# Moving tiles within a partition by 128 bytes, and placing the last output products by hand, in a hybrid decoder layer

## The chip, the core and the metric

The kernel is one Bass/Tile program on one core of a Trainium2 chip. The metric is the device time of one execution in microseconds (us). Five engines have work in it: TensorE (PE in the profile, with its weight loads listed apart as PEld), VectorE (DVE), ScalarE (ACT), GpSimd (POOL), and SyncE (SP), whose queue issues nearly all DMA transfers. Each engine takes its own instructions in a fixed order, which is settled when the program is built; a transfer at the head of SP's queue that has to wait holds up the ones behind it.

On-chip memory (SBUF) has 128 partitions. A tile takes the same byte range in each of them, so that "where a tile lies" is one byte address. A matmul reads two operands from there: the stationary one (128 columns, put into the array by a weight load ahead of the matmul) and the moving one (up to 512 columns, streamed through).

## What is computed

One decoder layer over x, 1024 tokens by 1024 features, float32:

```python
xn = rmsnorm(x, attn_norm_g)
proj = xn @ w_in                     # 2312 columns
# 8 sliding-window heads with sinks and ALiBi, 8 forgetting-attention heads, QK-norm in both
mixed = concatenate([out_a, out_b])  # 1024 columns
h = x + mixed @ w_out
y = h + square(relu(rmsnorm(h, mlp_norm_g) @ w_up)) @ w_down     # hidden width 4096
```

Each float32 operand of a large product is split into a high part (rounded to the type fp32r) and a low part (what is left), and each product is made of three matmuls: high by high, high by low, low by high.

## The kernel before

**Stages.** (1) Features of x come in eight blocks k; the first 384 columns of the projection are accumulated in eight PSUM banks `qps` (lines 168 to 191). (2) `load_w` brings further projection weights, `proj` makes the product `ps` of one block of 128 tokens (24 matmuls of 384 or 392 columns). The blocks are "fillers", handed out by the table `PACE` between the units of attention. (3) `heads_a` and `heads_b` run 48 attention units; a unit is a score step (`scores_a`, `scores_b`) and, two units later (`DEPTH`), a mix step (`mix_a`, `mix_b`), which transposes the probabilities, splits them (`evict_pt`) and multiplies them with the values (`pvb`). The list `marks` holds the last matmul of each score step. (4) The output product: `out_first` makes the half over e = 0 to 3 of all eight blocks dt of 128 output features while attention still runs; for dt = 0 and 4, e = 4 to 6 and then e = 7 are made at the end of attention (lines 862 to 875); the other six dt follow at lines 950 to 957. (5) `up`: 16 steps j of a Strassen-like product, seven products n of 12 matmuls of 512 columns each (`pu`). (6) `down`: 1344 matmuls of 512 columns (`pd`).

**Who sets the order.** Tile builds the program with a simulated timeline: at each step it takes the ready instruction of the highest priority. `tc.high_priority` raises what it wraps, `prep` uses it for attention; `tc.issue_after(ins)` queues what it wraps behind `ins` on that engine, which is a bound on the order and no wait; `paced()` is that with the newest mark. So an edit in one place can change the order of others.

**Where tiles lie.** The left side of memory holds the constants `cp` and behind them first x in its high and low parts (`xh`, `xl`, pool `xg_p`) with the projection weights (`wp`), later the pool `zl` (output weights, the attention outputs `mix`, up weights `wu`, part of what `down` uses). Sizes are rounded up to 32 bytes. Counted modulo 256 bytes, the constants begin at 128 and their odd-sized tiles put x and `zl` at 96. A projection weight tile has 392 floats, which is 6 times 256 bytes and 32 more, so that the eight high tiles and the eight low ones each begin 32 bytes further on, through all eight multiples of 32. The right side is filled from the end of memory: pools `ap1` and `ap2` for attention, later `zr` (the operands `bh` and `bl` of `up`, its sums, part of `down`). `zr` and its tiles lie at 224. In `ap2` small tiles stand between the large ones: q lies at 64, k and the split probabilities at 192.

**The attention outputs on their way to the output product.** `mix_b` (or `mix_a`) stores its result in `mix_d`. For each block e, `split_mix` loads it with its denominators (`mixr`, `mixn`, two tiles each), multiplies, splits into the one tile `mixs` (both parts; high on ACT, low on POOL), and stores 512 KB to `mixs_d`, once per half c. `load_mix(e)` brings the block back as `mix`. Its steps (load, half 0, half 1) are taken one per attention unit, from the units in `SPLITS`. Block e = 7 is split by `mix_b` directly.

Of the kernel before, what the change touches and what calls it, by code (L numbers as in the profile page):

```python
# [25 lines left out]
NJ = NF // 2  # L26
EPS = 1e-6
WN = 392
NW = 7
NWARM = 8  # L30
HPO = 8000
# [22 lines left out]
def hybrid_layer(  # L54
# [15 lines left out]
    def mm(out, lhsT, rhs, start, stop):  # L70
        return nc.tensor.matmul(out, lhsT, rhs, start=start, stop=stop)  # L71
# [29 lines left out]
    ones1 = cp.tile([P, 1], F32, name="ones1")  # L101
    nc.vector.memset(ones1, 1.0)

    vt = cp.tile([P, 36], F32, name="vt")
    nc.scalar.dma_start(vt, vecs)
    nc.scalar.preload_act_table_set("natural_log_exp_and_others")
    ga, gm, vec, bfb, snk = (
        vt[:, a:b] for a, b in ((0, 8), (8, 16), (16, 20), (20, 28), (28, 36))
    )
# [30 lines left out]
    at = ExitStack()  # L140
    ap1 = at.enter_context(tc.tile_pool(name="ap1", bufs=1, side="right"))
    ap2 = at.enter_context(tc.tile_pool(name="ap2", bufs=1, side="right"))
    maskd = ap2.tile([P, P], F32, tag="mt", name="maskd", bufs=2)
    nc.gpsimd.memset(maskd, 0.0)
    nc.gpsimd.affine_select(
# [4 lines left out]
    nc.vector.tensor_copy(mask_b, maskd)  # L150
    qk_t = lambda name: ap1.tile([P, NT, 384], F32, tag="qk", name=name, bufs=2)

    def w_tiles():
        return [
            wp.tile([P, WN], dt, tag=tag, name=tag, bufs=n)
            for tag, dt, n in (("wr", F32, 3), ("wh", F32R, 8), ("wl", F32R, 8))
        ]


    st0 = ExitStack()  # L160
# [6 lines left out]
    halves = [slice(c * 512, (c + 1) * 512) for c in range(2)]  # L167
    for k in range(KT):
        xr = ap2.tile([P, S], F32, tag="s", name="xr", bufs=NS)
        wr, wh, wl = w_tiles()  # L170
        nc.sync.dma_start(xr[:, halves[0]], xT[k * P : (k + 1) * P, halves[0]])
        nc.sync.dma_start(wr[:, :384], w_a0[:, k, :])
        nc.sync.dma_start(xr[:, halves[1]], xT[k * P : (k + 1) * P, halves[1]])
        split(wh[:, :384], wl[:, :384], wr[:, :384], nc.vector, nc.gpsimd if k else nc.vector)
        for cs in halves:
            nc.scalar.activation(xh[:, k, cs], xr[:, cs], AF.Copy, scale=ga[:, k : k + 1])
            nc.vector.scalar_tensor_tensor(
                out=xl[:, k, cs], in0=xr[:, cs], scalar=ga[:, k : k + 1],
                in1=xh[:, k, cs].bitcast(F32), op0=ALU.mult, op1=ALU.subtract,
            )  # L180
        passes = ((xh, wh), (xh, wl), (xl, wh))
        order = (
            [(t, j) for j in range(3) for t in range(NT)] if k == 0
            else [(t, j) for t in (range(NT) if k < KT - 1 else LAST) for j in range(3)]
        )
        for t, j in order:
            x_, w_ = passes[j]
            mm(
                qps[t][:, :384], x_[:, k, t * P : (t + 1) * P], w_[:, :384],
                k == 0 and j == 0, k == KT - 1 and j == 2,  # L190
            )
    q0 = qk_t("q0")
# [10 lines left out]
    def load_w(src, n):  # L203
        his, los = [], []
        for k in range(KT):
            wr, wh, wl = w_tiles()
            nc.sync.dma_start(wr[:, :n], src[:, k, :])
            with tc.high_priority(offset=HPO):
                split(wh[:, :n], wl[:, :n], wr[:, :n], nc.scalar, nc.gpsimd)
            his.append(wh)  # L210
            los.append(wl)
        return his, los
# [3 lines left out]
    def proj(w, n, t):  # L216
        his, los = w
        ps = pd.tile([P, 512], F32, tag="pd", name="ps")
        tsl = slice(t * P, (t + 1) * P)
        for k in range(KT):  # L220
            mm(ps[:, :n], xh[:, k, tsl], his[k][:, :n], k == 0, False)
            mm(ps[:, :n], xh[:, k, tsl], los[k][:, :n], False, False)
            pe = mm(ps[:, :n], xl[:, k, tsl], his[k][:, :n], False, k == KT - 1)
            if k == KT // 2:
                middle.append(pe.ins)
        return ps

    def qknorm(x, nh, tlo, thi, r=None):


        n = thi - tlo
        w = nh * HD
        sq = ap2.tile([P, 1024], F32, tag="sq", name="sq", bufs=1)
        sqv = sq[:, : n * w].rearrange("p (t c) -> p t c", t=n)
        xv = x[:, tlo:thi, :w]
        nc.gpsimd.tensor_tensor(out=sqv, in0=xv, in1=xv, op=ALU.mult)
        ss, r0, u = (
            ap2.tile([P, 16], F32, tag=tag, name=tag, bufs=2)[:, : n * nh]
            for tag in ("ss", "sr0", "su")
        )  # L240
        nc.vector.tensor_reduce(
            out=ss, in_=sq[:, : n * w].rearrange("p (g d) -> p g d", d=HD),
            axis=AX.X, op=ALU.add,
        )
        th = lambda a: a.rearrange("p (t h) -> p t h", h=nh)
        nc.vector.scalar_tensor_tensor(
            out=th(ss), in0=th(ss), scalar=1.0 / HD,
            in1=ep2[:, tlo:thi].unsqueeze(2).to_broadcast([P, n, nh]),
            op0=ALU.mult, op1=ALU.add,
        )  # L250
        nc.scalar.activation(r0, ss, AF.Ln)
        nc.scalar.activation(r0, r0, AF.Exp, scale=-0.5)
        nc.vector.tensor_tensor(out=u, in0=r0, in1=r0, op=ALU.mult)
        nc.vector.tensor_tensor(out=u, in0=u, in1=ss, op=ALU.mult)
        na = nh + (2 if r is not None else 0)
        if r is None:
            rv = ap2.tile([P, 16], F32, tag="r", name="r", bufs=2)[:, : n * nh]
            rv = th(rv)
        else:
            rv = r[:, tlo:thi, :]  # L260
        nc.vector.scalar_tensor_tensor(
            out=rv[:, :, :nh], in0=th(u), scalar=3.0, in1=th(r0),
            op0=ALU.subtract, op1=ALU.mult,
        )
        for t in range(n):
            xt = x[:, tlo + t, : na * HD].rearrange("p (h d) -> p h d", d=HD)
            nc.gpsimd.tensor_tensor(
                out=xt, in0=xt, in1=rv[:, t].unsqueeze(2).to_broadcast([P, na, HD]), op=ALU.mult
            )
# [153 lines left out]
    def forget_gates():  # L423
# [29 lines left out]
            off[: NH * NT, 0:1], before.rearrange("p h t -> p (h t)"),  # L453
            cum[:, P - 1 : P], True, True,
        )
        offs = ap2.tile([NH * NT, 1], F32, name="offs")
        nc.vector.tensor_copy(offs, off[: NH * NT, 0:1])
        nc.vector.tensor_scalar(
            out=cum, in0=cum, scalar1=offs[:, 0:1], scalar2=None, op0=ALU.add
# [96 lines left out]
    def split_mix(e):  # L556


        got = {}

        def load():
            for c in range(2):
                cs = slice(c * 512, (c + 1) * 512)
                m, q = got[c] = [
                    ap2.tile([P, 512], F32, tag=n, name=n, bufs=2) for n in ("mixr", "mixn")
                ]
                nc.sync.dma_start(m, mix_d[e][:, cs])
                for h in range(2):
                    nc.sync.dma_start(
                        q[rows_of[h], :], rd_d[2 * e + h, cs].partition_broadcast(HD)  # L570
                    )

        def make(c):
            m, q = got[c]
            hl = ap2.tile([P, 2, 512], F32R, tag="mixs", name="mixs", bufs=1)
            with tc.issue_after(mixed[-1]):
                nc.vector.tensor_tensor(out=m, in0=m, in1=q, op=ALU.mult)
            split(hl[:, 0], hl[:, 1], m, nc.scalar, nc.gpsimd)
            nc.sync.dma_start(
                mixs_d[e][:, :, c * 512 : (c + 1) * 512].rearrange("c p s -> p c s"),  # L580
                hl.bitcast(F32),
            )

        return [load, lambda: make(0), lambda: make(1)]

# [39 lines left out]
    def scores_b(p, qp, h):  # L625
        q1, k1, k2, cb = heads[p, "q"][h], heads[p, "k1", h], k2_of[h], heads[p, "cb", h]
        probs = []
        for i in (2 * qp, 2 * qp + 1):
# [2 lines left out]
                [P, S if i > 3 else 512], F32, tag="s" if i > 3 else "u", name="sb",  # L631
                bufs=NS if i > 3 else NU,
            )
            nm = ap2.tile([P, 4], F32, tag="nm", name="nmb", bufs=4)
            dn = ap2.tile([P, 4], F32, tag="dn", name="dnb", bufs=4)
            qs = q1[:, i * P : (i + 1) * P]
            for c in range((nk + 511) // 512):
                n = min(512, nk - c * 512)
# [32 lines left out]
    def mix_b(probs, p, qp, h):  # L671
        r = slice(h * HD, (h + 1) * HD)
        pv = pa.tile([P, 512], F32, tag="pv", name="pvb", bufs=2)
        for b in range(qp + 1):
# [18 lines left out]
            for par in range(2):  # L693
                st = heads[p, "v", h][:, 2 * b + par, :]
                mm(pvo, st, hv[:, :, 1 - par, :], b == 0 and par == 0, False)
                mm(pvo, st, lv[:, :, 1 - par, :], False, diag and par == 1)
        tmp = ap2.tile([HD, 512], F32, tag="cmb", name="tmpb", bufs=1)
        nc.scalar.copy(tmp[:, :256], pv[HD:, :256])
        mt = ap2.tile([P, 256], F32, tag="mt", name="mtb", bufs=2)
# [8 lines left out]
            split(mh[7][r, ms], ml[7][r, ms], mt[r, :], nc.scalar, nc.vector)  # L708

    qkb = {}  # L710
    mh, ml, mixt = {}, {}, {}
    pend = []

# [4 lines left out]
    def drain(n):  # L718
        while len(pend) > n:
            prep(pend.pop(0))  # L720
# [139 lines left out]
        heads_b(p)  # L860
    fill(True)
    load_mix(6)
    ahead_of = []
    for dt in (0, 4):
        w = out_weights(dt, 4)

        ps = first_banks() if dt == 0 else [
            pa.tile([P, 512], F32, tag="sc", name=f"po{c}", bufs=2) for c in range(2)
        ]
        with paced():  # L870
            out_products(ps, w, range(4, 7))
        ahead_of.append((dt, ps, w))
    drain(0)
    for dt, ps, w in ahead_of:
        out_products(ps, w, [7])

# [24 lines left out]
    def out_finish(dt, ps):  # L901
        t, gain = dt % 4, gm[:, dt : dt + 1]
        h = slot(f"w{2 + dt // 4}", "h", [S]) if dt < 7 else rr
        part["load"] = nc.sync.dma_start(h, part_d[dt])
        for c, cs in enumerate((left, right)):
            nc.vector.tensor_tensor(out=h[:, cs], in0=ps[c], in1=h[:, cs], op=ALU.add)
        nc.sync.dma_start(h_d[dt], h)
# [379 lines left out]
```

## Time and profile before

| | |
|---|---|
| median of 3 runs | 1126.16 us (1122.52 to 1127.7) |
| profiled execution | 1124.34 us, of which its span is 1122.6 us |
| granted TensorE clock, mean | 0.998 |
| matmuls | 5551, of which `pu` 1344, `pd` 1344, `ps` 960, `po` 384, `qps` 200 |

The profile is one execution. Busy time of PE is the union of its matmuls, which overlap: a matmul of 512 columns is listed with some 390 ns, but a new one starts every 230 ns or so. The rate is read from the chain of work that ended last, which merges matmuls that follow each other without a wait into one piece, with the piece's length and their number.

### The profile page before, as it was taken

The numbers are of one execution on the slowest core, as the hardware profiler recorded it, in microseconds if no ns is written. First come the engines' busy times: TensorE is split into PE (matmuls) and PEld (weight loads), VectorE is DVE, ScalarE is ACT, GpSimd is POOL, SyncE is SP. The second block draws the span as 40 slices with busy tenths as digits, with TensorE's granted clock in tenths as the row PEclk, the third lists the DMA queues.
The fourth block names the chain that finished last, engine by engine and source line by source line (L and its number), as shares of the span: only waits on it lengthen the run. The fifth ranks groups of instructions, "written<-read, shape, count | busy, mean of one in ns | idle before, by whom it ended". The sixth has DMA issues, their size and how long they took to land.

```text
span 1122.6 us, 15570 instructions
## 1 busy us (share of the span) xinstructions
PE 1098.7 (98%) x5551; PEld 937.5 (84%) x5551; DVE 765.4 (68%) x1311; ACT 575.4 (51%) x1013; POOL 361.0 (32%) x338
## 2 busy tenths in 40 slices
PE   9999998999999999899999999999999999999998
PEld 8999988799997888777888887888888888888886
DVE  7476665765667577699867677855575876674395
ACT  5567557766677656455454534344444433333331
POOL 4751613335434545124232323222221222222100
PEclk9999999999999999999999999999999999999999
DMA  9311302314438656473454544335699786665523
GB/s 312 124 36 37 95 24 59 96 29 142 153 120 312 203 182 219 168 236 131 173 194 169 196 151 159 134 121 194 227 392 351 258 299 244 216 230 205 173 95 113
DMA packets 95710, 195.68 MB, mean 174 GB/s; under 512 B 7136, under 2 KB 19088, under 8 KB 95632
## 3 DMA queue, kind: packets, MB, share of 16 engines
q1 hardware_dynamic: 95488, 194.66, 49.6%
q8 instruction: 44, 0.72, 0.3%
q14 instruction: 34, 0.28, 0.1%
q10 hardware_dynamic: 144, 0.02, 0.0%
HBM read 141.61 MB, written 53.04 MB: 173 GB/s over the span
## 4 chain that ended last, share of the span: by engine, by line
PE 83%; DVE 7%; issue 4%; DMA 4%; POOL 1%; ACT 1%; SPq 0%; DVEq 0%; ACTq 0%; POOLq 0%
PE pd L71 27%; PE pu L71 27%; PE ps L71 12%; PE po L71 4%; PE qps L71 3%; PE spb L71 3%; PE pvb L71 2%; PE tpb L683 2%; PE sp L71 1%; DVE ptl L360 1%; DMA mixs_d<-mixs 1%; DVE sb L647 1%; DVE bl L78 1%; PE pv L71 1%; DMA wr<-in_w_b_dram 1%
## 5 line engine op out<-in xcount | busy, mean ns | idle before, releaser
L71 PE MATMUL pd<-hx,wx 128*128 128x512 f32 x1344 | 304.9, 389 | 0.0
L71 PEld LDWEIGHTS pd<-hx,wx 128*128 128x128 f32 x1344 | 252.3, 188 | 52.4
L71 PE MATMUL pu<-bh,wu 128*128 128x512 f32 x896 | 281.6, 395 | 0.8 <-ACT wu L75 0.8
L71 PEld LDWEIGHTS pu<-bh,wu 128*128 128x128 f32 x896 | 168.8, 188 | 40.7 <-ACT wu L75 1.2
L71 PE MATMUL pu<-bl,wu 128*128 128x512 f32 x448 | 176.9, 395 | 0.5 <-DVE bl L78 0.5
L75 ACT CAST hx<-hr 128x1024 fp32r<-128x1024 f32 x56 | 59.0, 1054 | 176.2 <-PE pd L71 171.3
L78 POOL TENSOR_TENSOR wx<-wda,wx 128x1024 fp32r<-128x1024 f32 x24 | 64.5, 2687 | 197.0 <-ACT wx L75 197.0
L78 DVE TENSOR_TENSOR hx<-hr,hx 128x1024 fp32r<-128x1024 f32 x56 | 72.7, 1305 | 73.5 <-ACT hx L75 73.4
L71 PE MATMUL ps<-wh,xh 128*128 128x384 f32 (+1 forms) x320 | 110.2, 345 | 0.3 <-ACT qkb L600 0.3
L71 PE MATMUL ps<-wh,xl 128*128 128x384 f32 (+1 forms) x320 | 109.3, 342 | 0.0
L71 PE MATMUL ps<-wl,xh 128*128 128x384 f32 (+1 forms) x320 | 109.1, 342 | 0.0
L71 PEld LDWEIGHTS pu<-bl,wu 128*128 128x128 f32 x448 | 84.4, 188 | 21.1 <-DVE bl L78 0.9
L71 PE MATMUL po<-mix,wos 128*128 128x512 f32 x384 | 95.8, 400 | 3.7 <-DMA mix<-mixs_d 1.6
L78 POOL TENSOR_TENSOR wu<-wus,wu 128x512 fp32r<-128x512 f32 x32 | 48.0, 1501 | 133.4 <-ACT wu L75 133.4
L71 PEld LDWEIGHTS po<-mix,wos 128*128 128x128 f32 x384 | 70.9, 190 | 18.3 <-DMA mix<-mixs_d 1.8
L75 ACT CAST wu<-wus 128x512 fp32r<-128x512 f32 x64 | 39.0, 618 | 79.4 <-PE pu L71 76.0
L78 POOL TENSOR_TENSOR wu<-wur,wu 128x512 fp32r<-128x512 f32 x32 | 43.3, 1354 | 88.2 <-ACT wu L75 88.2
L360 DVE TENSOR_TENSOR ptl<-tpb,pth 128x512 fp32r<-128x512 f32 (+1 forms) x80 | 50.0, 632 | 25.9 <-ACT pth L359 25.2
L965 DVE TENSOR_TENSOR ht<-hb 128x512 f32<-128x512 f32 x32 | 21.8, 722 | 64.7 <-ACT hb L1020 64.7
L78 POOL TENSOR_TENSOR wl<-wr,wh 128x384 fp32r<-128x384 f32 (+1 forms) x47 | 49.9, 1076 | 48.8 <-ACT wh L75 36.9
L75 ACT CAST wx<-wda 128x1024 fp32r<-128x1024 f32 x56 | 58.3, 1044 | 7.2 <-DMA wda<-in_w_d_dram 6.6
L71 PEld LDWEIGHTS ps<-wh,xh 128*128 128x128 f32 x320 | 60.4, 189 | 1.1 <-ACT qkb L600 0.6
(218 smaller groups left out, 2058.4 us busy)
## 6 DMA issues: line engine op xcount, KB each, us to landing
wda<-in_w_d_dram SPq DMA_DIRECT2D x34, 1024.0 KB, 9.0
hr<-hid_d SPq DMA_DIRECT2D x56, 512.0 KB, 5.8
wur<-in_w_u_dram SPq DMA_DIRECT2D x32, 512.0 KB, 4.4
hid_d<-ht SPq DMA_DIRECT2D x16, 1024.0 KB, 4.3
hid_d<-hb SPq DMA_DIRECT2D x16, 768.0 KB, 3.6
mixs_d<-mixs SPq DMA_DIRECT2D x14, 512.0 KB, 3.4
mix<-mixs_d SPq DMA_DIRECT2D x7, 1024.0 KB, 8.7
wr<-in_w_b_dram SPq DMA_DIRECT2D x32, 192.0 KB, 2.4
```

The lines of the kernel that those rows point to most:

```text
L71: return nc.tensor.matmul(out, lhsT, rhs, start=start, stop=stop)
L75: hi_eng.copy(hi, src)
L78: lo_eng.tensor_tensor(out=lo, in0=src, in1=hi.bitcast(F32), op=ALU.subtract)
L360: nc.vector.tensor_tensor(out=lo[:, cols], in0=pt[:, cols], in1=hi[:, cols].bitcast(F32), op=ALU.subtract)
L647: nc.vector.tensor_tensor_reduce(out=pr[:, c * 512 : c * 512 + n], in0=sp[:, :n], in1=cb[:, c * 512 : c * 512 + n], scale=1.0, scalar=3e38 ...
L683: nc.tensor.transpose(tp[:, c0 : c0 + P], probs[qi][:, kb * P : (kb + 1) * P], ident)
L965: eng.tensor_tensor(out=out, in0=a, in1=b, op=ALU.subtract)
```

## The change

Seven edits:

1. `vt`, a tile of constants, grows from 36 to 68 floats. All that lies behind it on the left side moves by 128 bytes: x, the projection weights and the pool `zl` with the up weights. Modulo 256 they then begin at 224.
2. The high and low part of a projection weight go into one tile of 832 floats (13 times 256 bytes), the low one 1536 bytes behind the high one (1600 for the 392 columns of `w_a1`).
3. Small attention tiles go to a pool of their own, `ap3`, so that `ap2` holds only multiples of 256 bytes.
4. The first weight block is loaded from ACT's queue, and ACT's table load comes behind it.
5. `split_mix` writes the high part over the denominators `mixn`; `mixs` holds the low part alone, and each half is stored by two transfers.
6. At the end of attention, the products of dt = 0 and 4 over e = 4 to 6 are placed one by one behind a mark or behind the last matmul of a mix step (the list `ended`).
7. The partial sum of dt = 7 is loaded behind that of the block before it.

```diff
+WL = 416
...
-    vt = cp.tile([P, 36], F32, name="vt")
-    nc.scalar.dma_start(vt, vecs)
-    nc.scalar.preload_act_table_set("natural_log_exp_and_others")
+    vt = cp.tile([P, 68], F32, name="vt")
+    nc.scalar.dma_start(vt[:, :36], vecs)
...
+    ap3 = at.enter_context(tc.tile_pool(name="ap3", bufs=1, side="right"))
...
-    def w_tiles():
-        return [
-            wp.tile([P, WN], dt, tag=tag, name=tag, bufs=n)
-            for tag, dt, n in (("wr", F32, 3), ("wh", F32R, 8), ("wl", F32R, 8))
-        ]
+    def w_tiles(n):
+        w = wp.tile([P, 2 * WL], F32R, tag="w", name="w", bufs=8)
+        wr = wp.tile([P, WN], F32, tag="wr", name="wr", bufs=3)
+        lo = 384 if n == 384 else 400
+        return wr[:, :n], w[:, :n], w[:, lo : lo + n]
...
-        nc.sync.dma_start(wr[:, :384], w_a0[:, k, :])
+        (nc.sync if k else nc.scalar).dma_start(wr, w_a0[:, k, :])
+        if k == 0:
+            nc.scalar.preload_act_table_set("natural_log_exp_and_others")
...
-            ap2.tile([P, 16], F32, tag=tag, name=tag, bufs=2)[:, : n * nh]
+            ap3.tile([P, 16], F32, tag=tag, name=tag, bufs=2)[:, : n * nh]
...
                 m, q = got[c] = [
-                    ap2.tile([P, 512], F32, tag=n, name=n, bufs=2) for n in ("mixr", "mixn")
+                    ap2.tile([P, 512], dt, tag=n, name=n, bufs=2)
+                    for n, dt in (("mixr", F32), ("mixn", F32R))
                 ]
...
-            hl = ap2.tile([P, 2, 512], F32R, tag="mixs", name="mixs", bufs=1)
+            lo = ap2.tile([P, 512], F32R, tag="mixs", name="mixs", bufs=1)
...
-            split(hl[:, 0], hl[:, 1], m, nc.scalar, nc.gpsimd)
-            nc.sync.dma_start(
-                mixs_d[e][:, :, c * 512 : (c + 1) * 512].rearrange("c p s -> p c s"),
-                hl.bitcast(F32),
-            )
+            split(q, lo, m, nc.scalar, nc.gpsimd)
+            for part_, t in enumerate((q, lo)):
+                nc.sync.dma_start(
+                    mixs_d[e][part_][:, c * 512 : (c + 1) * 512], t.bitcast(F32)
+                )
...
-                mm(pvo, st, lv[:, :, 1 - par, :], False, diag and par == 1)
+                pe = mm(pvo, st, lv[:, :, 1 - par, :], False, diag and par == 1)
+        ended.append(pe.ins)
...
     for dt in (0, 4):
-        w = out_weights(dt, 4)
-
         ps = first_banks() if dt == 0 else [
             pa.tile([P, 512], F32, tag="sc", name=f"po{c}", bufs=2) for c in range(2)
         ]
-        with paced():
-            out_products(ps, w, range(4, 7))
-        ahead_of.append((dt, ps, w))
+        ahead_of.append((dt, ps, out_weights(dt, 4)))
+
+    def beside(n, mark, *es):
+        _, ps, w = ahead_of[n]
+        with tc.issue_after(mark):
+            out_products(ps, w, es)
+
+    beside(0, marks[-1], 4, 5)
+    beside(0, ended[-1], 6)
+    beside(1, ended[-1], 4)
+    drain(1)
+    beside(1, ended[-1], 5)
     drain(0)
+    beside(1, ended[-1], 6)
     for dt, ps, w in ahead_of:
         out_products(ps, w, [7])
...
-        part["load"] = nc.sync.dma_start(h, part_d[dt])
+        with tc.issue_after(part["load"].ins) if dt == 7 else nullcontext():
+            part["load"] = nc.sync.dma_start(h, part_d[dt])
```

The tiles `r`, `offs`, `nm` and `dn` go to `ap3` in the same way, and `load_w` and `proj` use the new tiles in place of `wh` and `wl`.

More of the change, by code (lines that the diff above doesn't have):

```diff
@@ L169, in hybrid_layer @@
         xr = ap2.tile([P, S], F32, tag="s", name="xr", bufs=NS)
-        wr, wh, wl = w_tiles()
+        wr, wh, wl = w_tiles(384)
         nc.sync.dma_start(xr[:, halves[0]], xT[k * P : (k + 1) * P, halves[0]])
-        nc.sync.dma_start(wr[:, :384], w_a0[:, k, :])
+        (nc.sync if k else nc.scalar).dma_start(wr, w_a0[:, k, :])
+        if k == 0:
+            nc.scalar.preload_act_table_set("natural_log_exp_and_others")
         nc.sync.dma_start(xr[:, halves[1]], xT[k * P : (k + 1) * P, halves[1]])
-        split(wh[:, :384], wl[:, :384], wr[:, :384], nc.vector, nc.gpsimd if k else nc.vector)
+        split(wh, wl, wr, nc.vector, nc.gpsimd if k else nc.vector)
         for cs in halves:
@@ L188, in hybrid_layer @@
             mm(
-                qps[t][:, :384], x_[:, k, t * P : (t + 1) * P], w_[:, :384],
+                qps[t][:, :384], x_[:, k, t * P : (t + 1) * P], w_,
                 k == 0 and j == 0, k == KT - 1 and j == 2,
@@ L205, in load_w @@
         for k in range(KT):
-            wr, wh, wl = w_tiles()
-            nc.sync.dma_start(wr[:, :n], src[:, k, :])
+            wr, wh, wl = w_tiles(n)
+            nc.sync.dma_start(wr, src[:, k, :])
             with tc.high_priority(offset=HPO):
-                split(wh[:, :n], wl[:, :n], wr[:, :n], nc.scalar, nc.gpsimd)
+                split(wh, wl, wr, nc.scalar, nc.gpsimd)
             his.append(wh)
@@ L220, in proj @@
         for k in range(KT):
-            mm(ps[:, :n], xh[:, k, tsl], his[k][:, :n], k == 0, False)
-            mm(ps[:, :n], xh[:, k, tsl], los[k][:, :n], False, False)
-            pe = mm(ps[:, :n], xl[:, k, tsl], his[k][:, :n], False, k == KT - 1)
+            mm(ps[:, :n], xh[:, k, tsl], his[k], k == 0, False)
+            mm(ps[:, :n], xh[:, k, tsl], los[k], False, False)
+            pe = mm(ps[:, :n], xl[:, k, tsl], his[k], False, k == KT - 1)
             if k == KT // 2:
@@ L256, in qknorm @@
         if r is None:
-            rv = ap2.tile([P, 16], F32, tag="r", name="r", bufs=2)[:, : n * nh]
+            rv = ap3.tile([P, 16], F32, tag="r", name="r", bufs=2)[:, : n * nh]
             rv = th(rv)
@@ L455, in forget_gates @@
         )
-        offs = ap2.tile([NH * NT, 1], F32, name="offs")
+        offs = ap3.tile([NH * NT, 1], F32, name="offs")
         nc.vector.tensor_copy(offs, off[: NH * NT, 0:1])
@@ L569, in load @@
                     nc.sync.dma_start(
-                        q[rows_of[h], :], rd_d[2 * e + h, cs].partition_broadcast(HD)
+                        q[rows_of[h], :].bitcast(F32), rd_d[2 * e + h, cs].partition_broadcast(HD)
                     )
@@ L574, in make @@
             m, q = got[c]
-            hl = ap2.tile([P, 2, 512], F32R, tag="mixs", name="mixs", bufs=1)
+            lo = ap2.tile([P, 512], F32R, tag="mixs", name="mixs", bufs=1)
             with tc.issue_after(mixed[-1]):
-                nc.vector.tensor_tensor(out=m, in0=m, in1=q, op=ALU.mult)
-            split(hl[:, 0], hl[:, 1], m, nc.scalar, nc.gpsimd)
-            nc.sync.dma_start(
-                mixs_d[e][:, :, c * 512 : (c + 1) * 512].rearrange("c p s -> p c s"),
-                hl.bitcast(F32),
-            )
+                nc.vector.tensor_tensor(out=m, in0=m, in1=q.bitcast(F32), op=ALU.mult)
+            split(q, lo, m, nc.scalar, nc.gpsimd)
[3 more added lines that the diff above has]
+                )
         return [load, lambda: make(0), lambda: make(1)]
@@ L633, in scores_b @@
             )
-            nm = ap2.tile([P, 4], F32, tag="nm", name="nmb", bufs=4)
-            dn = ap2.tile([P, 4], F32, tag="dn", name="dnb", bufs=4)
+            nm = ap3.tile([P, 4], F32, tag="nm", name="nmb", bufs=4)
+            dn = ap3.tile([P, 4], F32, tag="dn", name="dnb", bufs=4)
             qs = q1[:, i * P : (i + 1) * P]
@@ L710, in hybrid_layer @@
     qkb = {}
+    ended = []
     mh, ml, mixt = {}, {}, {}
```

## The prediction

> **What bounds the kernel now.** I read the page first: the busy times, then the chain of work that ended last. Its pieces show the rate at which TensorE takes matmuls where nothing interrupts it.
>
> ```profile
> PE 1098.7 (98%) x5551; PEld 937.5 (84%) x5551; DVE 765.4 (68%) x1311; ACT 575.4 (51%) x1013; POOL 361.0 (32%) x338
> ...
> 6.91 33.18 PE qps L71 x188
> 40.09 11.25 PE ps L71 x63
> ...
> 362.47 5.48 PE po L71 x24
> ...
> 512.40 181.77 PE pu L71 x781
> ...
> 695.88 117.12 PE pu L71 x504
> 813.01 300.64 PE pd L71 x1326
> ```
>
> The reader is to see two things. TensorE is busy for 98% of the span, so the time goes down only where its matmuls come closer together or where one of its few gaps closes. And the same matmul, 512 columns with 128 weights, does not always take the same: in `pu` (181.77 + 117.12) / 1285 = 232.6 ns, in `pd` 300.64 / 1326 = 226.7 ns, in `po` 5.48 / 24 = 228.3 ns. The order of parts (high, low, high) is the same in all three, and so is the engine's clock (1.00, below). What differs is where the operands lie: by the sizes of the tiles both operands of `po` are at 96 modulo 256 bytes, and both of `pd` are alike too (96 and 96, in a few steps 224 and 224), while in `pu` the weights are at 96 and the moving operand at 224. So the trace already holds the comparison on which most of the change rests: alike 226.7, 128 bytes apart 232.6, or 5.9 ns for each matmul.
>
> Next, the busy time by stretch, to see whether another engine would become the bound, and what the end of attention looks like.
>
> ```profile
> 520.00:690.00 170.00, 170.00 (x733) 137.88 (x732) 121.92 (x180) 81.29 (x102) 51.70 (x37) 1.00 0.48 174
> 820.00:1000.00 180.00, 180.00 (x796) 149.04 (x795) 130.83 (x109) 67.88 (x71) 44.28 (x16) 1.00 0.76 278
> ...
> 452.00:456.00 4.00, 4.00 (x16) 3.34 (x14) 0.00 (x0) 0.07 (x1) 0.00 (x0) 0.57 0.06 25
> ...
> 464.00:512.00 48.00, 47.12 (x203) 37.85 (x203) 46.69 (x63) 26.19 (x44) 15.65 (x11) 1.00 0.68 227
> ```
>
> The columns are length, then PE, PEld, DVE, ACT and POOL busy, then granted clock, DMA share and GB/s. In 520 to 690 (all `pu`) PE has no gap, DVE is busy for 72% and the DMA engines for 48%: a `pu` faster by 2.5% meets no other limit. In 464 to 512 it is otherwise: DVE is busy for 46.69 of 48 us, and a faster matmul there gains nothing.
>
> **The change, part by part.**
>
> *Up products.* The 128 bytes added to `vt` move the weights of `pu` from 96 to 224; its moving operand, filled from the other end of memory, stays at 224. Of the 1344 matmuls, 1285 stand in the pieces above where PE never waits; the other 59 fall into the stretch that DVE bounds and count nothing. 1285 x 5.9 ns = 7.5 us; I take 7.4, since the two closest like pairs, `pd` and `po`, differ by themselves (226.7 and 228.3; by `po` it would be 1285 x 4.3 = 5.5). `pd` and `po` move as a whole, both operands together, and gain nothing.
>
> [...]
>
> *Projection.* x is at 96 and its weights rotate through all multiples of 32; afterwards both are at 224 (the low part of the 392 columns is 64 bytes off). The trace has no stretch of 384 columns with all alike, so the cost is bounded. From here the rate for 256 columns:
>
> ```profile
> 459.58 0.28 PE L71 MATMUL pvb<-pth,vb 128*128 128x256 f32 x1
> 459.70 0.28 PE L71 MATMUL pvb<-ptl,vb 128*128 128x256 f32 x1
> 459.82 0.28 PE L71 MATMUL pvb<-pth,vb 128*128 128x256 f32 x1
> 459.94 0.28 PE L71 MATMUL pvb<-ptl,vb 128*128 128x256 f32 x1
> ```
>
> They start 0.36 / 3 = 0.12 us apart. Half way between that and 226.7 ns lies 173.4 ns, my estimate for 384 columns with operands alike. `qps` now takes 33.18 / 188 = 176.5 and `ps` 11.25 / 63 = 178.6 (some of these with 392 columns). The most is therefore 1152 x 3.1 ns = 3.6 us, the least 0, if the turning offsets cost nothing on average. I take half, 1.8 us, since some of the 176.5 is small waits, and since `ps` in attention shares PE with chains that it does not set.
>
> *Attention.* Its own products become alike too. Only the widest score matmuls can show it:
>
> ```profile
> L71 PE MATMUL spb<-k1b,q1b 128*128 128x512 f32 x48 | 20.6, 430 | 0.6 <-DVE nmb L647 0.6
> ```
>
> With the same number for the low parts these are 96; at 5.9 ns at most 0.6 us, at least 0; I take 0.3.
>
> *The start.* The weight load leaves SP's queue, and the second half of x moves up by one place.
>
> ```profile
> 1.24 0.42 SPq L172 DMA_DIRECT2D wr<-in_w_a_dram  x1
> 1.71 0.42 SPq L173 DMA_DIRECT2D xr<-in_xT_dram  x1
> ...
> 1.23 1.28 ACT L106 ACT_TABLE_LOAD   x1 [1.23 <-PEq L1270]
> 3.84 0.72 ACT L176 ACTIVATE xh<-xr,vt 128x512 fp32r<-128x512 f32 x1 [1.32 <-DMA vt<-in_vecs_dram]
> 6.14 0.72 ACT L176 ACTIVATE xh<-xr,vt 128x512 fp32r<-128x512 f32 x1 [1.58 <-DMA xr<-in_xT_dram]
> ...
> 6.91 0.97 PE L71 MATMUL qps<-wh,xh 128*128 128x384 f32 x4 [0.62 <-ACT xh L176]
> ```
>
> PE stands for 0.62 us because the second half of x came late; that half is now issued 1.71 - 1.24 = 0.47 us sooner. The table load is put back by one issue, some 0.4 us, and stays hidden: ACT has 1.32 us to spare until `vt` lands at 3.84. I take 0.4, between 0 (the transfers share the same engines) and 0.62. Where that cover is gone, it costs the same 0.4.
>
> *The end of attention.* Here are PE's gaps, and the chain that leads to the first:
>
> ```profile
> 451.69 3.34 PE L71 MATMUL po<-mix,wos 128*128 128x512 f32 x8 [1.58 <-DMA mix<-mixs_d]
> ...
> 461.62 1.64 PE L71 MATMUL po<-mix,wos 128*128 128x512 f32 x6 [1.40 <-ACT mix L75]
> 463.95 6.44 PE L71 MATMUL po<-mix,wos 128*128 128x512 f32 x27 [0.69 <-ACT wos L75]
> ...
> 436.05 5.80 DMA mixs_d<-mixs
> ...
> 441.92 0.63 ACT mixs L75
> 442.55 0.07 issue
> 442.62 1.30 POOL mixs L78
> 443.92 0.02 issue
> 443.94 2.74 DMA mixs_d<-mixs
> ...
> 446.74 4.90 DMA mix<-mixs_d
> ```
>
> At 450 PE has used up its filler products (e = 4 and 5 of both blocks) and waits 1.58 us for block e = 6; then the clock falls to half (0.57 in 452 to 456), and eight matmuls take 3.34 us where 8 x 0.227 = 1.8 would do: some 1.6 us lost. Later it waits 1.40 us for the last mix step to be split. Together 4.6 us; the 0.69 behind them waits for weights and stays. The new placing puts six matmuls (1.4 us) right behind the last mix step, into the gap of 1.40, and keeps 12 (2.7 us) for after the third-last one, so that PE has work when the load is late. The load itself comes sooner: the high half of c = 1 no longer waits for the store of c = 0 (0.63 + 0.07 us), and the last store is 256 KB in place of 512. What still waits: the low half, on POOL, for the store of the low half before it, since `mixs` keeps one buffer. I take the 1.40 in full and half of the other 3.2: 3.0 us. The bounds are 4.6, and a loss of 1.4, if PE, which takes its instructions in order, meets e = 6 of dt = 0 ahead of its data while products that are ready stand behind it.
>
> [...]
>
> *The rest.*
>
> ```profile
> L579 SPq DMA_DIRECT2D mixs_d<-mixs x14: 370/376/383, 252.9 to 443.9; - x14
> ```
>
> Fourteen more stores are issued on SP, at 0.376 us each, 5.3 us spread over 252.9 to 443.9, in a queue that nothing on the path stands behind for so long: nothing. The new wait is that a denominator load into `mixn` must let the high part's store land; behind it on SP stand the stores of `mix_d`, weight loads `wr` and, for whoever waits, the fillers of PE. It is the rival on the other side. The load for dt = 7, moved behind another on SP, is wanted only after 500 us.
>
> *Sum:* 7.4 + 1.8 + 0.3 + 0.4 + 3.0 = 12.9 us. The profiled execution took 1124.34 us (span 1122.6 and 1.74 around it), so 1111.4; the median of the runs shown is 1.8 us above that execution, which puts the forecast at **1113 us**. With all terms at their best 7.5 + 3.6 + 0.6 + 0.6 + 4.6 = 16.9, or 1109; with `pu` by the rate of `po` and the rest at the least, but the gap of 1.40 closed, 6.9, or 1119.
>
> **The rivals.**
>
> *The order costs.* Step 6 goes wrong as said, and 1.4 us are lost where 3.0 were counted: 12.9 - 4.4 = 8.5, 1118 us. For it speaks that the load landed at 451.64 and PE ran dry at 450.1 with twice the filler ahead of it; against it, that the builder places what is ready first in its own timeline.
>
> *Place does not matter*, or the tiles do not come to lie as I worked out: the terms of 7.4, 1.8 and 0.3 are gone, 3.4 us are left, 1123 us. For it stands that `pu` and `pd` also differ in what ACT, POOL and the transfers do beside them; against it, that `po`, with yet other company, agrees with `pd` and not with `pu`.
>
> *SP blocked by the new wait: slower.* Its place is the load step of `split_mix`, its price the landing of a store:
>
> ```profile
> mixs_d<-mixs SPq DMA_DIRECT2D x14, 512.0 KB, 3.4
> ```
>
> If each of the 14 halves held SP's queue for 3.4 us and PE's fillers starved for as long, 47.6 us would be added; the change turns slower once more than 12.9 / 3.4, about four halves, are exposed in full. Seven of them (one for each block) would give 23.8 - 12.9 = 10.9 more, 1137 us. Against it speaks that the steps of one block are a unit apart and the next block starts two units later or more, so the store has long landed.
>
> **How the numbers follow.** Forecast 0.70; the order costs 0.13; place does not matter 0.08; SP blocked 0.04; 0.05 for a different order of attention throughout, either way. The range goes from 1107 (the best sum and a little luck in the order) to 1120 (the second case with `pu` by the rate of `po`): it leaves out the last three, 0.17. A measurement of this kernel tells about 0.5% (5.6 us) from no change. Faster by more than that, below 1120.5: 0.70 + 0.13 + 0.03 = 0.86; within it 0.10; slower 0.04.
>
> **What would show it.** `pu` in the chain at about 226.7 ns a matmul, its stretch shorter by 7 us, with `pd` still at 226.7; `qps` near 174; no gap at `po` over 1 us and no half clock around 450; PE's first long piece starting near 6.5 us. A `pu` that stays at 232 would end the first step; a gap at `po` ahead of e = 6, the last one; long waits of `wl` or `wh` for `wr` between 200 and 440 us would speak for a blocked SP.

## The result, and the profile after

The changed kernel takes 1114.55 us (median of 6 runs, 1111.68 to 1116.15) against 1127.09 us before on the same chips: ratio 0.989, 95% interval 0.9867 to 0.9913. The forecast was 1113, the range 1107 to 1120. The profiled execution of the changed kernel took 1111.68 us, its span 1110.0 us. Times compared here are of undisturbed executions; one of the kernel before, 1818.11 us at a granted clock of 0.556, is left out.

First the chain of work that ended last, of the kernel after (start, length, what, number of instructions):

```profile
507.35 177.36 PE pu L72 x781
...
686.42 114.29 PE pu L72 x504
800.72 300.57 PE pd L72 x1326
```

These are the same pieces as before, with the same numbers of matmuls. `pu` went from 298.89 us to 177.36 + 114.29 = 291.65, or 227.0 ns a matmul in place of 232.6; `pd` stayed at 226.7, with both operands, by the tile sizes, at 96 before (in a few steps 224) and at 224 after: it isn't the place of one operand alone that counts. That is 7.2 us.

Next TensorE in order of time at the end of attention, after (start, length, engine, line, instruction, number, and in brackets the idle time before it):

```profile
447.36 1.64 PE L72 MATMUL po<-mix,wos 128*128 128x512 f32 x6
...
449.66 1.64 PE L72 MATMUL po<-mix,wos 128*128 128x512 f32 x6
...
451.25 1.55 PE L72 MATMUL po<-mix,wos 128*128 128x512 f32 x6
...
455.16 3.59 PE L72 MATMUL po<-mix,wos 128*128 128x512 f32 x15
459.44 2.79 PE L72 MATMUL po<-mix,wos 128*128 128x512 f32 x11 [0.69 <-ACT wos L76]
```

The gaps of 1.58 and 1.40 us are gone in this execution: groups of six output matmuls stand between the last mix steps, and the last mix step is followed by 15 of them in one piece. Only the 0.69 us wait for weights is left, 4.5 us earlier than before (459.44 for 463.95). By stretches, from the last score matmul to the first long piece of `pu`, before and after:

```profile
438.00:512.40 74.40, 69.25 (x323) 56.13 (x322) 61.72 (x93) 38.84 (x71) 18.09 (x18) 0.98 0.57 193
```

```profile
437.80:507.30 69.50, 67.06 (x323) 54.98 (x321) 61.58 (x93) 38.76 (x71) 18.77 (x18) 1.00 0.61 206
```

The same 323 matmuls take 4.9 us less; TensorE's idle time in it went from 5.15 us to 2.44, and part of the rest is the half clock that before had at 452 (0.98 mean clock).

Last, the start and the first score product, after and before:

```profile
6.75 3.04 PE L72 MATMUL qps<-w,xh 128*128 128x384 f32 x16 [1.87 <-DVE w L78]
...
36.85 0.19 ACT L379 ACTIVATION_READ_ACCUMULATOR xq<-xq 128x1 f32 x1
...
58.78 0.38 PE L72 MATMUL sp<-k1a,q1a 128*128 128x256 f32 x1 [0.41 <-DVE q1a L289]
```

```profile
36.13 0.18 ACT L371 ACTIVATION_READ_ACCUMULATOR xq<-xq 128x1 f32 x1
58.06 0.39 PE L71 MATMUL sp<-k1a,q1a 128*128 128x256 f32 x1
```

The start did not get better: TensorE waits 1.87 us for the first weight split, where before it waited 0.47 and 0.62. VectorE, before and after, shows why: the split (`wh`, now `w`) stands behind three products of the bias table `ab` before, and behind all eight after:

```profile
4.25 0.69 DVE L397 TENSOR_SCALAR ab<-dist 128x256 f32<-128x256 f32 x3
4.86 0.35 DVE L77 CAST wh<-wr 128x384 fp32r<-128x384 f32 x1
```

```profile
4.63 1.70 DVE L405 TENSOR_SCALAR ab<-dist 128x256 f32<-128x256 f32 x8
6.25 0.35 DVE L78 CAST w<-wr 128x384 fp32r<-128x384 f32 x1
```

Attention begins 0.72 us later, which is no more than two traces of one order differ by (58.06 us before, 59.01 with edit 1 alone). In the stretch from there to the last score product (58.78 to 437.78, before 58.06 to 437.94) the kernel wins that back.

### The profile page after: what moved, and what is told of

Its sections match the earlier page's. It is cut to its first block, busy times and chain, and to the rows that moved or that the text cites. A ratio compares the mean times of both kernels' runs of the same rounds, so it can differ in the third digit from the quotient of the medians.

```text
span 1110.0 us, 15616 instructions
## 1 busy us (share of the span) xinstructions
PE 1087.6 (98%) x5551; PEld 934.2 (84%) x5551; DVE 770.4 (69%) x1311; ACT 573.1 (52%) x1013; POOL 361.6 (33%) x338
## 4 chain that ended last, share of the span: by engine, by line
PE 82%; DVE 9%; DMA 3%; issue 3%; ACT 2%; POOL 1%; SPq 0%; DVEq 0%; ACTq 0%; POOLq 0%
PE pd L72 27%; PE pu L72 26%; PE ps L72 12%; PE po L72 5%; PE spb L72 3%; PE pvb L72 3%; PE tpb L692 2%; PE sp L72 1%; DMA xq<-in_x_dram 1%; DVE ptl L368 1%; PE pv L72 1%; PE tpa L527 1%; DVE bl L79 1%; DVE sb L656 1%; DVE bl L918 1%
## 5 line engine op out<-in xcount | busy, mean ns | idle before, releaser
L72 PE MATMUL pu<-bh,wu 128*128 128x512 f32 x896 | 276.6, 390 | 0.4 <-ACT wu L76 0.4
L72 PE MATMUL pu<-bl,wu 128*128 128x512 f32 x448 | 174.4, 390 | 0.8 <-DVE bl L79 0.8
L72 PE MATMUL ps<-w,xh 128*128 128x384 f32 (+1 forms) x640 | 173.4, 342 | 0.3 <-ACT qkb L609 0.3
L76 ACT CAST hx<-hr 128x1024 fp32r<-128x1024 f32 x56 | 59.0, 1054 | 175.8 <-PE pd L72 171.2
L72 PEld LDWEIGHTS ps<-w,xh 128*128 128x128 f32 x640 | 114.9, 189 | 1.3 <-ACT qkb L609 0.6
L72 PE MATMUL ps<-w,xl 128*128 128x384 f32 (+1 forms) x320 | 109.0, 341 | 0.0
L72 PEld LDWEIGHTS po<-mix,wos 128*128 128x128 f32 x384 | 69.9, 188 | 14.5 <-ACT wos L76 1.1
L79 POOL TENSOR_TENSOR w<-wr,w 128x384 fp32r<-128x384 f32 (+1 forms) x47 | 50.0, 1079 | 49.3 <-ACT w L76 36.5
L367 ACT CAST pth<-tpb 128x512 fp32r<-128x512 f32 (+1 forms) x80 | 43.2, 544 | 34.7 <-PE tpb L692 30.1
```

The costliest lines, as they stand in the source:

```text
L76: hi_eng.copy(hi, src)
L79: lo_eng.tensor_tensor(out=lo, in0=src, in1=hi.bitcast(F32), op=ALU.subtract)
L367: nc.scalar.copy(hi[:, cols], pt[:, cols])
```

## The experiments

Of eleven runs, four tell whether distance sets the rate of `pu`, two what the placing is worth, two what the start does, two the projection; one was to beat the kernel after. Where "same order" is said, the built programs have each engine's instructions in the same order as the kernel they are compared with, so that only addresses differ.

**Edit 1 alone** (same order as before):

```diff
-    vt = cp.tile([P, 36], F32, name="vt")
-    nc.scalar.dma_start(vt, vecs)
+    vt = cp.tile([P, 68], F32, name="vt")
+    nc.scalar.dma_start(vt[:, :36], vecs)
```

> The kernel before with edit 1 alone: vt has 68 floats, so x, the projection weights and the up weights all lie 128 bytes further on. If the distance between the two operands of a matmul modulo 256 bytes sets the rate: pu in the chain at 226.8 ns a matmul instead of 232.6, the kernel 7 to 8 us faster than before (ratio 0.993 to 0.994), the end of attention with its gaps of 1.6 and 1.4 us as before, the projection unchanged (x and its weights move together and still rotate against each other). If where tiles lie does not matter and something else in the change made pu faster: pu stays at 232 and the time within 1 us of before.

Measured: 1116.8 us, ratio 0.9922 (0.9907 to 0.9937). The chain of this kernel:

```profile
511.67 177.32 PE pu L71 x781
...
690.71 114.29 PE pu L71 x504
805.00 300.57 PE pd L71 x1326
```

291.61 us for the 1285 matmuls, the same as after to 0.04 us, from 128 bytes in a tile of constants. The gaps at the end of attention are as before (2.08 and 1.40 us):

```profile
452.60 2.11 PE L71 MATMUL po<-mix,wos 128*128 128x512 f32 x8 [2.08 <-DMA mix<-mixs_d]
```

The theory of distance holds, and the rest of the change has no part in `pu`.

**The other distances**, on the kernel after, by the size of `vt` (same order as after):

```diff
-    vt = cp.tile([P, 68], F32, name="vt")
+    vt = cp.tile([P, 60], F32, name="vt")    # 52 and 36 in the other two
```

> The kernel after with vt at 60 floats in place of 68, so that the weights of pu lie 32 bytes in front of its moving operand modulo 256, all else alike. If any distance but 0 costs the same: pu at 232 to 233 ns a matmul. If the cost grows with the distance: 228 to 229. If only a distance of 128 costs: 226.8. pd and qps, whose two operands move together, stay at 226.7 and 173.5 in every case.

> The same with vt at 52 floats: 64 bytes apart. Any distance costs the same: 232 to 233 ns a matmul. Cost grows with the distance: 229 to 230. Only 128 costs: 226.8.

> The same with vt at 36 floats, as before: 128 bytes apart. If distance is all that changed for pu: 232.4 to 232.7 ns a matmul again and 7 to 8 us on the up stage, while qps (x and its weights at 96 both) stays at 173.5 as after. If something else in the change made pu faster: 226.8.

Measured, from the chains, 32, 64 and 128 bytes apart:

```profile
512.41 182.49 PE pu L72 x781
...
696.62 117.60 PE pu L72 x504
814.22 300.73 PE pd L72 x1326
```

```profile
510.82 179.05 PE pu L72 x781
...
691.58 117.60 PE pu L72 x504
```

```profile
510.54 182.49 PE pu L72 x781
...
694.75 117.12 PE pu L72 x504
```

| bytes apart | 0 (after) | 32 | 64 | 128 |
|---|---|---|---|---|
| ns per matmul of `pu` | 227.0 | 233.5 | 230.9 | 233.2 |

Each of these distances costs 4 to 6.5 ns, 32 bytes as much as 128, and 64 a little less on the whole, between the values expected. So it isn't a cost that grows with the distance. Nor does the distance alone set its size: at 64 bytes one execution shows 229.3 ns up to the wait between the two pieces and 233.3 behind it, which I can't explain. `pd` and `qps`, whose operands move together, stay at 226.7 to 226.8 and 173.3 to 173.5. One execution of each took 1125.39, 1120.29 and 1122.91 us. Since 32, 64 and 128 bytes all cost, the period is none of these; that it is 256 bytes and not a multiple of it, no run tests.

**The placing**, alone on the kernel before, and undone on the kernel after:

```diff
-        with paced():
-            out_products(ps, w, range(4, 7))
-        ahead_of.append((dt, ps, w))
+        ahead_of.append((dt, ps, out_weights(dt, 4)))
...
+    beside(0, marks[-1], 4, 5)
+    beside(0, ended[-1], 6)
+    beside(1, ended[-1], 4)
+    drain(1)
+    beside(1, ended[-1], 5)
     drain(0)
+    beside(1, ended[-1], 6)
```

> The kernel before with edit 6 alone. If the placing closes the gaps by itself: 3 to 4.5 us less than before, the half clock around 452 gone, the up stage as before at 232.6 ns a matmul. If it needs the earlier load of e = 6: a wait for the transfer of block 6 of 1 us or more stays in front of its products, and the gain is 1 to 2 us.

> The kernel after with edit 6 undone: the last output products stand in the order of before, all behind the last score step. If the placing by hand closed the gaps at the end of attention: the wait of about 1.4 us for the last mix step comes back, and with it a wait of 0 to 1.6 us for block e = 6, in all 1.4 to 4.5 us more than after. If the earlier load of e = 6 (edits 5 and 7) did it: at most 1 us more than after.

Measured: alone 1122.18 us, ratio 0.9972 (0.996 to 0.9983); undone 1118.58 us, ratio 0.9942 (0.9927 to 0.9957). TensorE's waits at this place, first with the placing alone, then with it undone:

```profile
461.09 2.11 PE L71 MATMUL po<-mix,wos 128*128 128x512 f32 x8 [0.69 <-ACT wos L75]
```

```profile
452.00 3.04 PE L72 MATMUL po<-mix,wos 128*128 128x512 f32 x12 [1.82 <-DMA mix<-mixs_d]
...
462.61 0.73 PE L72 MATMUL po<-mix,wos 128*128 128x512 f32 x2 [1.46 <-ACT mix L76]
```

With the placing alone both gaps are gone, though block 6 is stored and loaded as before; without it both are there, though block 6 is stored in halves. So the order of TensorE closes them, and edits 5 and 7 do not. They did not even bring the load forward: block 6 has landed 12.8 to 14.5 us behind the last score product in the ten traces with edit 5, and 13.7 to 14.2 in the three without. Edit 5 also frees 2 KB in each partition, and edit 2's weight tiles take 1.5 KB; undoing edit 5 alone was not tried.

Over all traces of these runs, from the last score matmul to the first long piece of `pu`: 74.5, 73.3 and 74.3 us without the placing (before, edit 1 alone, placing undone), 69.6 to 71.8, mean 70.6, in the ten with it. The difference of the means is 3.4 us, which is what the placing is worth; the 4.9 between the two profiles is a good draw after and a half clock before. The waits are not quite gone either: in seven of the ten traces TensorE still waits 0.16 to 0.62 us for block 6.

**The start.** Edit 4 undone on the kernel after; and edit 4 kept, with the work that stands in front of the first split moved behind it:

```diff
-        (nc.sync if k else nc.scalar).dma_start(wr, w_a0[:, k, :])
-        if k == 0:
-            nc.scalar.preload_act_table_set("natural_log_exp_and_others")
+        nc.sync.dma_start(wr, w_a0[:, k, :])
```

> The kernel after with edit 4 undone: the first weight block on SP again, ACT's table load in front. After, TensorE waits 1.87 us for the first weight split, where before it had two waits of 0.47 and 0.62 with four matmuls between. If the start of the change costs what that shows: the first attention products about 0.7 us sooner, and 0 to 0.7 us off the end, since by 150 us only 0.1 us of the late start was left. If the start is unrelated to edit 4: no difference at 60 us.

```diff
+    with tc.issue_after(first_lo.ins):     # the low part of the first weight split
         for h in range(NH):
             nc.vector.tensor_scalar_mul(ab[h // 4][:, h % 4, :], dist, 2.0 ** -(h + 1))
```

> The kernel after with one addition: the eight VectorE products of the bias table ab (1.70 us, in front of the first weight split after) are queued behind that split. If they are what makes TensorE wait 1.87 us at the start: that wait falls to 0.7 us or less, and no half clock falls on the first 11 us. For the end of the span: if the start of attention hangs on TensorE, 1 to 1.5 us less than after; if it hangs on the loads and VectorE work that lead to the first scores, those still start near 58.8 us and the time is within 0.7 us of after, save that the executions in which the clock was halved early get 1.5 us faster.

Measured: 1111.94 us, ratio 0.9884 (0.9869 to 0.99), and 1114.71 us, ratio 0.9904 (0.9876 to 0.9931). Neither can be told from the kernel after. The second, in order of time:

```profile
5.75 3.01 PE L72 MATMUL qps<-w,xh 128*128 128x384 f32 x16 [0.87 <-ACT xh L186]
...
38.08 0.18 ACT L381 ACTIVATION_READ_ACCUMULATOR xq<-xq 128x1 f32 x1
...
59.97 0.39 PE L72 MATMUL sp<-k1a,q1a 128*128 128x256 f32 x1 [0.41 <-DVE q1a L291]
```

TensorE starts 1.0 us sooner than after (its wait fell to 0.87 us, now for `xh`, and not to the 0.7 expected), and the first score product comes 1.2 us later. With edit 4 undone it comes at 59.38 us, 0.6 later than after; 0.7 sooner was expected if edit 4 set it. What the first score product follows is the last block of x in its row layout (`xq`, loaded a second time for the sums of squares): from the start of ScalarE's last step on it to the first score product it is 21.9 us in the three kernels whose lines are shown (36.13 to 58.06, 36.85 to 58.78, 38.08 to 59.97). I expected scores near 58.8; they came at 59.97 since `xq` came later, why is open. The 21.9 us hold in eleven of the thirteen traces. In the other two (32 bytes apart, and the kernel after once more) they are 23.3 and 22.4, and TensorE's projection products run without a wait up to the first score product.

The late split also goes with something that the profile of the kernel after doesn't show. In four of the eight traces that have it (these two, 64 bytes apart, and placing undone) the first 16 matmuls of `qps` take 4.57 to 5.46 us in place of 3.04, most of them 320 ns apart in place of 173; with the placing undone the profile gives a granted clock of 0.68 from 6 to 10 us, with the kernel after once more one of 1.00 from 5 to 10. In none of the five traces in which the first of these matmuls starts by 5.75 us are they so slow. What this costs at the end the medians do not show.

**The projection.** The weight tiles turning against x again, all else as after (same order); and the kernel after once more on the same chip:

```diff
-        w = wp.tile([P, 2 * WL], F32R, tag="w", name="w", bufs=8)
+        w = wp.tile([P, 2 * WN], F32R, tag="w", name="w", bufs=8)
...
-        lo = 384 if n == 384 else 400
+        lo = WN
```

> The kernel after with edit 2's spacing undone: a weight tile has 784 floats, its low part 392 floats in, so that the weights of the projection turn against x by multiples of 32 bytes as before; each engine's instructions are in the same order as after. If the projection's rate sets its time: qps back at 175 to 176 ns and ps near 175.8, and 0.6 to 1.8 us more than after. If TensorE's rate there is hidden by the loads and chains that set the pace of attention: the same rates, but first scores and last scores of attention as after within 0.3 us, and no difference in time.

> The kernel after once more, on the same chip as the two runs above, as their measure: 0.9890 of before (0.9867 to 0.9913). pu at 226.8 ns a matmul in any execution; the gap of 1.72 us at 339 in any; a half clock in some place or none, by execution.

Measured: turning 1115.46 us, ratio 0.9904 (0.989 to 0.9917); after again 1114.86 us, ratio 0.99 (0.9887 to 0.9914). The mean distance from one matmul's start to the next, where they follow without a wait, is in `qps` 175.1 ns before, 174.3 turning and 173.5 after; in `ps` (384 and 392 columns together) 175.8, 176.3 and 175.1 to 175.3. So the rate is there, but it is 0.7 to 1.6 ns a matmul, and it makes 0.9 us (190 x 1.6 + 803 x 0.7 ns). The times of these two runs differ by 0.6, which is inside their intervals, so that whether the rate reaches the end of the kernel isn't shown. In `qps` I expected 175 to 176 from turning weights: they bring back half of the difference to before, and where the other half comes from is open.

**An attempt to beat the kernel after.** In every trace here but one, TensorE waits 1.72 us near 340 us for a split on VectorE, behind a multiplication of 0.69 and a reduction of 1.2 us:

```diff
-                nc.vector.tensor_tensor(out=m, in0=m, in1=q.bitcast(F32), op=ALU.mult)
+                (nc.gpsimd if e < 6 else nc.vector).tensor_tensor(
+                    out=m, in0=m, in1=q.bitcast(F32), op=ALU.mult
+                )
```

> The kernel after with one product moved: the multiplication by the denominators in split_mix, 0.69 us each, goes from VectorE to GpSimd for e = 0 to 5. It stands with a reduction of 1.2 us in front of the split that TensorE waits 1.72 us for at 339 us, a wait that is in the trace of before and of after alike and after which some executions show half the clock for 3.4 us. If that wait is one of VectorE's queue: it falls to about 1.0, the half clock near 342 goes, and the time is 0.7 to 2 us under after. If the transfers and ScalarE set it: no difference.

Measured: 1125.04 us, ratio 0.9993 (0.9982 to 1.0005); ten us slower than after. TensorE, GpSimd and ScalarE in order of time, then the busy times by stretch (clock third from the end):

```profile
248.49 0.58 PE L72 MATMUL pvb<-pth,vb 128*128 128x256 f32 x1 [4.14 <-ACT pth L367]
...
245.94 1.26 POOL L586 TENSOR_TENSOR mixr<-mixr,mixn 128x512 f32<-128x512 f32 x1 [2.96 <-DMA mixn<-rd_d]
...
247.23 0.62 ACT L76 CAST mixn<-mixr 128x512 fp32r<-128x512 f32 x1 [3.10 <-POOL mixr L586]
...
247.88 0.95 ACT L367 CAST pth<-tpb 128x512 fp32r<-128x512 f32 x2
```

```profile
246.00:254.00 8.00, 5.47 (x22) 4.27 (x22) 4.55 (x13) 4.33 (x9) 5.03 (x8) 0.57 0.39 134
```

On VectorE the multiplication is queued behind a mix step, and TensorE has no such wait in the kernel after (0.20 us at most from 236 to 256 us); on GpSimd nothing holds it back. It stands in its queue for 2.96 us waiting for `mixn`, ScalarE's high part waits behind it (3.10 us), the split of the probabilities `pth` behind that, and TensorE for 4.14 us, after which its clock is at half for 6.8 us. The same happens once more at 369.8 us, with a wait of 2.66 us for `pth` and a half clock of 3.4 us. From the first score product to the last it is 389.6 us in place of 379.0, which is 10.6 us more and the whole loss. The wait at 340 did go from 1.72 to 1.12 us.

## Why the prediction was right, point by point

**Up products: right, also in size.** Forecast 7.4 us, measured 7.2 in the profile, 7.3 in the chain of edit 1 alone (8.6 in its times, 1125.4 - 1116.8, whose interval holds 7.3). That operands alike modulo 256 bytes are fast is shown by the four distances, 227.0 ns against 230.9 to 233.5, so the rival by which place does not matter failed; that 256 is the period is worked out from where the tiles lie and not tested. What in the memory makes the difference no run shows.

**Projection: mechanism right, size half.** The estimate of 173.4 ns with operands alike was met in `qps` (173.5). The term was too large because its starting point, 176.5 and 178.6 from two pieces of the chain, held small waits and matmuls of 392 columns; matmul by matmul it was 175.1 in `qps` and, for 384 columns alone, 174.9 in `ps` before. In `ps` the estimate was not met: 174.3 after. By the rates it is 0.9 us in place of 1.8, and no time shows it.

**Attention products: nothing.** 0.3 us were counted. The spacing of the widest score matmuls did not fall (in the median 234 ns before, 235 after).

**Start: the sign was wrong.** The step that failed is "that half is now issued 0.47 us sooner". It was, but the weight split came behind all eight products of `ab` on VectorE in place of three, a reordering by the builder that the diff does not show. The medians show no cost at the end, since the first scores follow `xq` and not TensorE in most traces; but the late split goes with a slow first stretch of TensorE in four traces of eight, which the forecast did not count.

**End of attention: right.** Forecast 3.0 us, within bounds of -1.4 and 4.6; 3.4 over the traces, 3.2 in the times of the placing alone (1125.4 - 1122.18). Of the reasons given, the load of block 6 that "comes sooner" failed: it came no sooner, and the order closed the gaps without it. The reading "some 1.6 us lost" to the half clock was too high as well: a listed piece holds its last matmul in full, and the same eight are listed with 2.11 us where the clock did not fall (edit 1 alone), so 3.34 - 2.11 = 1.2 us were lost.

**Rivals.** The order cost little: TensorE does meet e = 6 ahead of its data in seven of ten traces, but waits 0.62 us at most (0.50 in the kernel with turning weights), and not at all in the one shown. SP was not blocked: in the profile after, it stands 0.8 us in all for a store ahead of the loads into `mixn`, and TensorE's idle time between 200 and 438 us is 6.5 us, before 6.4. The sum of the parts, 7.2 + 0.9 + 3.4 = 11.5 us, holds 0.9 that only the rates show; the medians say 12.5 in one set of runs and 11.2 (1126.02 - 1114.86) in the other. That the forecast of 12.9 came so near is in part luck: its three small terms, 2.5 us together, came out as 0.9, and the placing as 0.4 more than forecast.

## What to carry to other kernels

Before looking for gaps, compare the rates of like matmuls between stages; where one stage is slower, compare where the two operands lie (here 227.0 ns a matmul with both alike modulo 256 bytes, 230.9 to 233.5 with 32 to 128 bytes between them), and shift a pool by padding one tile. Work that is ready early belongs in the places where an in-order engine would wait, not ahead of all of them (3.4 us here). And an edit to a kernel whose order a builder makes is priced by the new order: look at it before believing the gain, as the multiplication on GpSimd and the split at the start showed.

## What was not expected of the hardware

**A distance of 32 bytes costs as much as 128** (233.5 and 233.2 ns). At 64 it costs less for a time: 229.3 ns, and after a wait 233.3, in one execution.

**The half clock came in one execution and not in another.** The same wait of 1.72 us near 340 is followed by half the clock in one and not in the other; of the six traces with the order of the kernel after, three have it. Between executions of one kernel the mean clock differs too, from 0.996 to 1.000 in sixteen of the kernel before. The stretch behind it, first of the kernel with edit 4 undone, then of the kernel after (clock third from the end):

```profile
342.00:347.00 5.00, 5.00 (x26) 4.33 (x27) 4.75 (x14) 2.79 (x7) 2.77 (x8) 0.66 1.02 415
```

```profile
342.00:347.00 5.00, 4.66 (x34) 3.78 (x33) 4.97 (x16) 3.53 (x7) 3.41 (x6) 1.00 1.02 414
```

The clock is 0.66 in the one and 1.00 in the other. Edit 1 alone had a wait of 2.08 us at 450 without it (1.00 from 452 to 456); before, 1.58 us with it (0.57). Near 342 the half clock lasted 3.4 us and delayed what followed by about 1.1 us: from the last matmul of `ps` to the last score product it is 104.0 to 104.2 us in the six traces that had it there, and 102.9 to 103.1 in the six that had not (the kernel with the multiplication on GpSimd left aside). It makes part of the spread from 1111.68 to 1116.15 us, and a term of the forecast that counts on it, like the 1.6 us at the end of attention, is a chance and not a cost.
